# Free bytes between SBUF tiles: other offsets modulo 512 bytes between the moving tiles and the weights of a float32r transformer trunk

## The chip, the core and the metric

The kernel runs on one core of one Trainium2 chip. The metric is the device time of one execution in microseconds (us). Times are medians over repeated executions; one execution is also recorded by the hardware profiler, and all rows below come from that one.

## The reference

Two layers of a transformer trunk over 256 latent tokens and 256 context tokens, model width 1024, float32. Each layer is a half-step SwiGLU feed-forward, an attention (layer 0 differential attention, layer 1 GQA with normed queries and keys), and a second half-step feed-forward; a conditioning vector shifts, scales and gates every branch. Cut to what matters:

```python
def swiglu(h, w_in, w_out):                       # w_in 1024 x 5632, w_out 2816 x 1024
    gate, up = jnp.split(h @ w_in, 2, axis=-1)
    return (jax.nn.silu(gate) * up) @ w_out

for i in range(2):
    mod = (silu(c) @ w_mod[i] + b_mod[i])         # 9 vectors of 1024, also for the context
    x  = x + 0.5 * mod[2] * swiglu(modulate(x, norm_g[i, 0], mod[0], mod[1]), w_ffn_in[i, 0], w_ffn_out[i, 0])
    xc = ...                                      # the same for the context tokens
    h  = modulate(x, norm_g[i, 1], mod[3], mod[4])
    x  = x + mod[5] * attention_i(h, hc)          # 0: differential, 1: GQA
    x  = x + 0.5 * mod[8] * swiglu(modulate(x, norm_g[i, 2], mod[6], mod[7]), w_ffn_in[i, 1], w_ffn_out[i, 1])
return rms_norm(x, final_g)
```

In layer 1 the context stops after the attention, so the last feed-forward has 256 tokens only.

## The kernel before

All 512 tokens lie along the free axis and features along the 128 partitions. Nearly all the work is matrix products on TensorE. Each float32 operand is split into a high part (rounded to float32r) and a low part (the rest), and a product is three float32r matmuls, written by `mac` (lines 384 to 386):

```python
        nc.tensor.matmul(out, ah, bh, start=first, stop=False)
        nc.tensor.matmul(out, ah, bl, start=False, stop=False)
        return nc.tensor.matmul(out, al, bh, start=False, stop=last)
```

The first of the two inputs is the stationary one: 128x128 values loaded into the array by a weight load. The second is the moving one: up to 512 columns that stream through it. The profile writes `gate<-hhi,whi` with the moving tile first. A weight load reads 512 bytes of each partition and runs under the matmul before it; a moving operand of 512 columns reads 2048 bytes of each partition.

The weights come from memory in pieces: `advance` (line 137) loads each into `raw`, ScalarE rounds it to `whi` (line 150), VectorE subtracts to get `wlo` (line 151). They are the stationary operand everywhere but in the value projections, where the normed activations are stationary and the weights move. The kinds of moving tiles are:

- `hhi`, `hlo` (`h_hi`, `h_lo`): the normed input of a stage, 8 tiles of 512 columns each. They feed `gate` and `up` of the feed-forwards, `g` (the first products of a feed-forward) and the projections `qk`, `q`, `k` of the attentions; in `v` they are stationary.
- `ahi`, `alo`: the 11 hidden tiles of one half of a feed-forward. They feed `out`, and `e` at the end of a stage.
- `pa`: attention outputs, which feed `op`.
- `ks`, `kl`: stacked keys, which move against stacked queries `qs` in the scores `sps` (lines 630 and 631).

Products run in the order in which they are written: for each of the 22 column blocks of a feed-forward `gate` and `up` with 8 x 3 matmuls each, then `out` with 11 x 3 matmuls for each pair of output tiles. In differential attention (`diff_attention`, line 674) the tile framework's scheduler interleaves each head's scores, exponentials and transposes with the next head's projections. There `outputs` (line 767) squares the four blocks of a head's output with ScalarE (line 781) into a scratch tile `osq`, of which there is one.

Tiles lie in SBUF in the order in which their pools and tags are first asked for, each pool behind the last, each tile rounded up to 32 bytes. Nothing in the code before fixes an address, and the sizes before `h_hi` are such that, in the built program, weights and moving tiles start at these bytes modulo 512 in each partition (slices of a tile start whole multiples of 512 bytes further on):

| tiles | start modulo 512 before | relative to the weights' 160 |
|---|---|---|
| `whi`, `wlo` | 160 | 0 |
| `hhi`, `hlo` | 160 | 0 |
| `ahi`, `alo` | 32 | 384 |
| `pa` of differential attention | 96 | 448 |
| `kl` / `ks`, `qs` of differential attention | 96 / 352 | 448 / 192 |
| `pa`, `ks`, `kl`, `qs` of GQA | 32 | 384 |

Of the kernel before, what the change touches and what calls it, by code (L numbers as in the profile page):

```python
# [11 lines left out]
F32 = mybir.dt.float32  # L12
F32R = mybir.dt.float32r
# [6 lines left out]
P = 128  # L20
D = 1024
KD = D // P
SEQ = 256
CTX = 256
T = SEQ + CTX
# [18 lines left out]
PIECE_AT = (18, 21, 24, 26, 28, 31, 32, 33)  # L44
WARM = 24


@with_exitstack
def trunk(ctx: ExitStack, tc: tile.TileContext, a: dict):
    nc = tc.nc  # L50
    PSUM = bass.MemoryType.PSUM

    const = ctx.enter_context(tc.tile_pool(name="const", bufs=1))
    wpool = ctx.enter_context(tc.tile_pool(name="wpool", bufs=2))
    stat = ctx.enter_context(tc.tile_pool(name="stat", bufs=1))
    tmp = ctx.enter_context(tc.tile_pool(name="tmp", bufs=3))
# [6 lines left out]
    def ax_tile(name):  # L63
        return ax_ps.tile([P, 512], F32, tag="ax", name=name)


    tok = (slice(0, SEQ), slice(SEQ, T))

    sck = tmp.tile([P, KD, 32], F32, tag="sq", name="sck")
# [65 lines left out]
    def raw_tile(name):  # L135
        return wpool.tile([P, 1024], F32, tag="raw", name=name, bufs=5)

    def advance(upto):
        for i in range(len(ready), min(upto, len(flat) - 1) + 1):
            src, pieces, f = flat[i]  # L140
            parts, c0 = [], 0
            for q, kt in enumerate(pieces):
                n = kt * f
                raw = raw_tile(f"raw{i}_{q}")
                nc.sync.dma_start(raw[:, :n], src[:, c0 : c0 + n])
                hi = wpool.tile([P, 1024], F32R, tag="whi", name=f"whi{i}_{q}", bufs=6)
                lo = wpool.tile([P, 1024], F32R, tag="wlo", name=f"wlo{i}_{q}", bufs=6)
                step = n // 2 if i in fine else n
                for c in (slice(b, b + step) for b in range(0, n, step)):
                    nc.scalar.activation(hi[:, c], raw[:, c], AF.Copy)  # L150
                    nc.vector.tensor_tensor(lo[:, c], raw[:, c], hi[:, c].bitcast(F32), op=ALU.subtract)  # L151
                parts += [(hi[:, k * f : k * f + f], lo[:, k * f : k * f + f]) for k in range(kt)]
                c0 += n
            ready[i] = parts

    def weight(i, look=LOOK):
        advance(i + look)
        return ready[i]
# [165 lines left out]
    def table(func, after):  # L324

        t = tmp.tile([P, 1], F32, tag="tab", name="tab")
        return nc.scalar.activation(t, after, func, scale=0.0, bias=1.0)

    h_hi = [stat.tile([P, T], F32R, name=f"hhi{j}", tag=f"hhi{j}") for j in range(KD)]
    h_lo = [stat.tile([P, T], F32R, name=f"hlo{j}", tag=f"hlo{j}") for j in range(KD)]  # L330

    def modulated_tile(l, n3, s, j, rstd, eng=nc.vector):
# [98 lines left out]
    def boundary(groups, nxt, follow):  # L431


        for s in range(2):
            for i, (outs, ends, tiles) in enumerate(groups):
                ps = [mm_tile(f"e{t}") if t < 3 and not (s and i) else ax_tile(f"e{t}") for t in range(tiles)]
                outs(ps, tok[s])
                if s and i == len(groups) - 1:
                    advance(nxt)
                ends(ps, s)  # L440
            if s:
                advance(nxt + 1)
            steps.extend(modulated(*follow, s))
            if s == 0:
                norm_step()
                norm_step()


    def ffn(l, s, n, follow=None, f_steps=0, o_steps=0, upto=(0, 0)):
# [4 lines left out]
        nxt = base  # L454
        with ExitStack() as st:
            fp = st.enter_context(tc.tile_pool(name=f"ffn{l}{s}", bufs=2))
            a_hi = [fp.tile([P, T], F32R, tag=f"ahi{i}", name=f"ahi{i}", bufs=1) for i in range(NH)]
            a_lo = [fp.tile([P, T], F32R, tag=f"alo{i}", name=f"alo{i}", bufs=1) for i in range(NH)]

            def load_sc(after=None):  # L460
# [33 lines left out]
            for hf in range(2):  # L494
                i0 = 0
                if hf == 0 and opening:
                    i0 = G0
                    with tc.tile_pool(name="open", bufs=2) as sp:
# [7 lines left out]
                        for k in range(KD + 2):  # L506
# [8 lines left out]
                            if k > 1:  # L515
                                w = ready[nxt + k - 2]
# [12 lines left out]
                elif hf == 0:  # L529
                    i0 = 2  # L530
                    banks = [mm_tile(f"g{b}") if b < 3 else ax_tile(f"g{b}") for b in range(4)]
                    w = [weight(nxt, 1), weight(nxt + 1, 0)]
# [15 lines left out]
                for i in range(i0, NH):  # L548
                    w = weight(nxt)
# [9 lines left out]
                for jj in range(0, KD, 2):  # L559
# [18 lines left out]
                    w = [weight(nxt), weight(nxt + 1, 0 if final else LOOK)]  # L578
# [97 lines left out]
    def diff_attention(l):  # L676
        base = start["att", l]
        scale = 64 ** -0.5
        with tc.tile_pool(name="da", bufs=2) as ap:
            lam = ap.tile([P, 4], F32, tag="lam", name="lam", bufs=1)  # L680
            nlam = lam[:, 3:4]
            g1 = ap.tile([P, 1], F32, tag="g1", name="g1", bufs=1)

            lamv = tmp.tile([P, 4, 64], F32, tag="ht", name="lamv")
            for i, n in enumerate(("da_lam_q1", "da_lam_k1", "da_lam_q2", "da_lam_k2")):
                nc.scalar.dma_start(lamv[:, i, :], a[n].to_broadcast([P, 64]))

            kls = [[ap.tile([P, T], F32R, tag=f"kl{i}{m}", name=f"kl{i}{m}", bufs=1) for m in range(2)] for i in range(2)]
            for kl in kls:
                zero_others(kl)  # L690

            def lambdas(after):
                lj = ap.tile([P, 64], F32, tag="lj", name="lj", bufs=1)
                for i in range(2):
                    nc.vector.tensor_tensor_reduce(
                        out=lj, in0=lamv[:, 2 * i, :], in1=lamv[:, 2 * i + 1, :], op0=ALU.mult, op1=ALU.add,
                        scale=1.0, scalar=0.0, accum_out=lam[:, i : i + 1],
                    )
                table(AF.Exp, after)
                nc.scalar.activation(lam[:, 0:2], lam[:, 0:2], AF.Exp)  # L700
                nc.vector.tensor_tensor(lam[:, 2:3], lam[:, 1:2], lam[:, 0:1], op=ALU.subtract)
                nc.vector.tensor_scalar(nlam, lam[:, 2:3], -LAM_INIT, None, op0=ALU.add)
                nc.vector.tensor_scalar(g1, subln_g, 1.0 - LAM_INIT, None, op0=ALU.mult)

            pa = [[ap.tile([P, T], F32R, tag=f"pa{i}{k}", name=f"pa{i}{k}", bufs=1) for k in range(4)] for i in range(2)]

            def v_mac(ps, w, k, s_, t):
                c = slice(s_ * 256 + t * P, s_ * 256 + t * P + P)
# [58 lines left out]
            def outputs(hd):  # L767
                ops = ax_tile("ops")
                h = hd["h"]
                for u in range(4):  # L770
                    k0 = 0 if u < 2 else 2
                    for kt in range(k0, 4):
                        nc.tensor.matmul(
                            ops[:, u * P : u * P + P], hd["pT"][u][:, kt - k0, :],
                            hd["v"][:, kt, (h % 2) * P : (h % 2) * P + P], start=kt == k0, stop=kt == 3,
                        )
                o, ms = hd["o"], hd["ms"]
                nc.vector.tensor_copy(o[:, :, h % 2, :], ops.rearrange("p (t f) -> p t f", t=4))
                for u in range(4):
                    osq = ap.tile([P, P], F32, tag="osq", name="osq", bufs=1)  # L780
                    nc.scalar.activation(
                        osq, ops[:, u * P : u * P + P], AF.Square, accum_out=ms[:, u, h % 2 : h % 2 + 1]
                    )
# [26 lines left out]
            def behind(hd, u):  # L810

                turned(hd, u)
                if u == U_AT and done:
                    pair = done.pop()
                    scaled(pair)
                    h = pair["h"]
                    if h < HEADS // 2:
                        parts_of(pair, o_hi[h - 1 : h + 1], o_lo[h - 1 : h + 1])
                    else:
                        late.append(pair)  # L820
                if u == 3:
                    outputs(hd)
                    if hd["h"] % 2:
                        normed(hd)
                        done.append(hd)
# [44 lines left out]
            for s_ in range(2):  # L870
# [5 lines left out]
                for k in range(KD):  # L876
                    for g in range(2):
                        mac(
                            qkps[g][:, tok[s_]], w_part(wqk, k, slice(g * P, g * P + P)), h_part(k, tok[s_]),
                            k == 0, k == KD - 1,  # L880
                        )
            lambdas(last_norm["rstd"][:, 0:1])
            v_tile(0)
            for t in range(2):
# [27 lines left out]
    def gqa(l):  # L912
        base = start["att", l]
        scale = 64 ** -0.5
        with tc.tile_pool(name="gq", bufs=2) as ap:
            qs = [ap.tile([P, SEQ], F32R, tag=f"qs{i % 8}", name=f"qs{i}", bufs=1) for i in range(16)]
            ks = [ap.tile([P, T], F32R, tag=f"ks{i}", name=f"ks{i}", bufs=1) for i in range(4)]
            kl = [ap.tile([P, T], F32R, tag=f"kl{i}", name=f"kl{i}", bufs=1) for i in range(4)]
# [3 lines left out]
            pa = [[ap.tile([P, SEQ], F32R, tag=f"pa{i}{k}", name=f"pa{i}{k}", bufs=1) for k in range(8)] for i in range(2)]  # L922
# [136 lines left out]
            for n, un in enumerate(units + [None, None]):  # L1059
                if un:  # L1060
                    flight.append((un, weights_of(*un)))
                if n in Q_AT:
                    i, g = divmod(Q_AT.index(n), 2)
# [8 lines left out]
                if n in sqs:  # L1072
                    i, sq = sqs[n]
# [11 lines left out]
            out_proj(base + 8, range(4, 8), o_part, l, SEQ, 1, (l, 2))  # L1085

    ffn(0, 0, T, (0, 1), 2, 1, (0, 7))
    diff_attention(0)
    ffn(0, 1, T, (1, 0), 1.5, 1, (1, 1))
    ffn(1, 0, T, (1, 1), 1.5, 1, (1, 8))  # L1090
    gqa(1)
    ffn(1, 1, SEQ)

# [102 lines left out]
```

## Time and profile before

| | us |
|---|---|
| median of 2 runs | 1729.39 (1728.10 to 1730.68) |
| the profiled execution, its time | 1729.97 |
| its span, first to last instruction | 1727.8 |
| TensorE matmuls busy | 1707.0 |
| VectorE busy | 1159.4 |
| ScalarE busy | 730.3 |
| granted share of the TensorE clock | 0.996 |

Busy times of matmuls overlap, since each is recorded from its start until its last result, while the next has already begun. So the pace of TensorE is read from the distance between the starts of neighbouring matmuls, in the timeline view, and not from the duration of one. Below, "step" means that distance. The timeline's columns are start (us), duration (us), engine, line, operation, output and inputs, shape, and in brackets idle time before it with what ended it.

### The profile page before, as it was taken

The page shows a single profiled execution, that of the slowest core. Times are in us where ns is not written, and L with a number is a line of the kernel's source. Part 1 is how long each engine was busy: PE and PEld are TensorE (multiplying, and loading weights), DVE is VectorE, ACT ScalarE, POOL GpSimd, SP SyncE. Part 2 cuts the span into 40 slices and gives each one's busy share as a digit, 9 for nine tenths or more (in the row PEclk, how much of TensorE's full clock was granted, in tenths as well). Part 3 has the DMA queues.
Part 4 walks back from the last instruction along what each step waited for, and adds up shares of the span by engine and source line. Part 5 has one row for each costly group of instructions (what it writes and reads, how often), then busy time and mean ns, then how long its engine had stood idle before and what let it go on. Part 6 is the DMA issues. An engine that isn't in the chain of part 4 may idle for free.

```text
span 1727.8 us, 24899 instructions
## 1 busy us (share of the span) xinstructions
PE 1707.0 (99%) x9586; PEld 1463.1 (85%) x9586; DVE 1159.4 (67%) x2113; ACT 730.3 (42%) x1359; POOL 26.3 (2%) x42
## 2 busy tenths in 40 slices
PE   9999999999999999999999999999999999999998
PEld 6788888789888889888888898888888897799998
DVE  3697777756888868756766557545543488876664
ACT  3432222235767646322222244222222368765454
POOL 0000000000100000000000000000000010000000
PEclk8999999999999999999999999999999999999999
DMA  7675565442122223545644535546552332145652
GB/s 255 228 242 160 187 215 161 153 151 101 57 67 74 73 74 123 179 140 160 203 156 150 169 110 183 152 132 196 178 160 77 118 101 72 50 164 146 217 162 83
DMA packets 76870, 249.59 MB, mean 144 GB/s; under 512 B 9936, under 2 KB 10064, under 8 KB 76752
## 3 DMA queue, kind: packets, MB, share of 16 engines
q1 hardware_dynamic: 75456, 247.25, 44.9%
q8 instruction: 75, 1.23, 0.3%
q10 hardware_dynamic: 1296, 0.76, 0.1%
q14 instruction: 43, 0.35, 0.1%
HBM read 246.92 MB, written 1.05 MB: 144 GB/s over the span
## 4 chain that ended last, share of the span: by engine, by line
PE 84%; DVE 7%; issue 3%; DMA 2%; ACT 2%; POOL 0%; DVEq 0%; ACTq 0%; POOLq 0%
PE out L385 7%; PE out L386 7%; PE out L384 7%; PE gate L384 7%; PE gate L385 7%; PE gate L386 7%; PE up L385 7%; PE up L386 7%; PE up L384 7%; DMA wm<-in_w_mod 2%; PE g L384 2%; PE g L385 2%; PE g L386 2%; DVE junk L172 1%; PE e L384 1%
## 5 line engine op out<-in xcount | busy, mean ns | idle before, releaser
L150 ACT ACTIVATE whi<-raw 128x1024 fp32r<-128x1024 f32 (+3 forms) x426 | 350.4, 836 | 455.7 <-PE out L385 248.5
L151 DVE TENSOR_TENSOR wlo<-raw,whi 128x1024 fp32r<-128x1024 f32 (+3 forms) x426 | 399.6, 946 | 186.5 <-ACT whi L150 185.7
L172 DVE CUSTOM_DVE_ANT_0 junk<-wm,sc,b_mod 128x1024 bf16<-128x1024 f32 x224 | 287.4, 1283 | 186.4 <-DMA wm<-in_w_mod 182.8
L384 PE MATMUL gate<-hhi,whi 128*128 128x512 f32 (+1 forms) x648 | 234.0, 361 | 0.7 <-DVE av L474 0.7
L386 PE MATMUL gate<-hhi,wlo 128*128 128x512 f32 (+1 forms) x648 | 233.7, 361 | 0.0
L385 PE MATMUL gate<-hlo,whi 128*128 128x512 f32 (+1 forms) x648 | 233.6, 361 | 0.0
L385 PE MATMUL up<-hlo,whi 128*128 128x512 f32 (+1 forms) x648 | 233.6, 361 | 0.0
L384 PE MATMUL up<-hhi,whi 128*128 128x512 f32 (+1 forms) x648 | 233.6, 360 | 0.0
L386 PE MATMUL up<-hhi,wlo 128*128 128x512 f32 (+1 forms) x648 | 233.5, 360 | 0.0
L385 PE MATMUL out<-alo,whi 128*128 128x512 f32 (+1 forms) x638 | 232.3, 364 | 0.0
L384 PE MATMUL out<-ahi,whi 128*128 128x512 f32 (+1 forms) x638 | 232.0, 364 | 0.0
L386 PE MATMUL out<-ahi,wlo 128*128 128x512 f32 (+1 forms) x638 | 231.8, 364 | 0.0
L402 ACT ACTIVATE ahi<-av 128x512 fp32r<-128x512 f32 (+1 forms) x88 | 50.7, 578 | 211.8 <-DVE av L474 204.5
L384 PEld LDWEIGHTS gate<-hhi,whi 128*128 128x128 f32 x648 | 122.4, 189 | 20.2 <-DVE av L474 1.6
L385 PEld LDWEIGHTS out<-alo,whi 128*128 128x128 f32 x638 | 119.9, 188 | 21.4 <-DVE alo L403 0.4
L386 PEld LDWEIGHTS gate<-hhi,wlo 128*128 128x128 f32 x648 | 122.4, 189 | 18.4
L385 PEld LDWEIGHTS up<-hlo,whi 128*128 128x128 f32 x648 | 122.4, 189 | 18.4
L384 PEld LDWEIGHTS up<-hhi,whi 128*128 128x128 f32 x648 | 122.4, 189 | 18.4
L386 PEld LDWEIGHTS up<-hhi,wlo 128*128 128x128 f32 x648 | 122.4, 189 | 18.3
L385 PEld LDWEIGHTS gate<-hlo,whi 128*128 128x128 f32 x648 | 122.4, 189 | 18.2
L386 PEld LDWEIGHTS out<-ahi,wlo 128*128 128x128 f32 x638 | 119.7, 188 | 21.1
L384 PEld LDWEIGHTS out<-ahi,whi 128*128 128x128 f32 x638 | 119.8, 188 | 21.0
(240 smaller groups left out, 2618.0 us busy)
## 6 DMA issues: line engine op xcount, KB each, us to landing
raw<-in_w_in SPq DMA_DIRECT2D x170, 512.0 KB, 4.4
wm<-in_w_mod SPq DMA_DIRECT2D x128, 512.0 KB, 4.2
raw<-in_w_out SPq DMA_DIRECT2D x64, 384.0 KB, 3.4
raw<-in_w_out SPq DMA_DIRECT2D x64, 320.0 KB, 3.1
raw<-in_da_vqk SPq DMA_DIRECT2D x24, 512.0 KB, 3.9
wf<-in_w_mod SPq DMA_DIRECT2D x16, 512.0 KB, 5.0
raw<-in_gq_qkv SPq DMA_DIRECT2D x12, 512.0 KB, 3.8
raw<-in_da_o SPq DMA_DIRECT2D x8, 512.0 KB, 3.7
```

What stands on the lines that cost most here:

```text
L150: nc.scalar.activation(hi[:, c], raw[:, c], AF.Copy)
L151: nc.vector.tensor_tensor(lo[:, c], raw[:, c], hi[:, c].bitcast(F32), op=ALU.subtract)
L172: nc.vector.tensor_tensor_reduce(out=junk, in0=raw, in1=mod_pool["sc"][:, s, :], op0=ALU.mult, op1=ALU.add, scale=1.0, scalar=b_mod[:, l, ...
L384: nc.tensor.matmul(out, ah, bh, start=first, stop=False)
L385: nc.tensor.matmul(out, ah, bl, start=False, stop=False)
L386: return nc.tensor.matmul(out, al, bh, start=False, stop=last)
L402: nc.scalar.activation(hi, src, AF.Copy)
```

## The change

`gap` allocates a tile that nothing uses. Such free bytes go in front of `h_hi` (256) and `h_lo` (320), in front of `ahi` (128) and `alo` (64) in each feed-forward, and in front of `kl` (32) and the second list of `pa` (64) in differential attention. To make the pools' other tiles not disturb the sums, `lam` and `g1` move from the attention's pool to the general pool `tmp`, the small scratch tile `lj` takes the place of `sw`, and `osq` becomes a slice of `sq`, of which there are three.

```diff
+GAPS = dict(const=0, w=0, norm=(256, 320), ffn=(128, 64), da=(32, 64), gq=0)
...
+    def gap(pool, i, n):
+
+        if n:
+            pool.tile([P, n // 4], F32, tag=f"gap{i}", name=f"gap{i}", bufs=1)
...
+    lam = tmp.tile([P, 4], F32, tag="lam", name="lam", bufs=1)
+    nlam = lam[:, 3:4]
+    g1 = tmp.tile([P, 1], F32, tag="g1", name="g1", bufs=1)
+
+    gap(stat, 0, GAPS["norm"][0])
     h_hi = [stat.tile([P, T], F32R, name=f"hhi{j}", tag=f"hhi{j}") for j in range(KD)]
+    gap(stat, 1, GAPS["norm"][1])
     h_lo = [stat.tile([P, T], F32R, name=f"hlo{j}", tag=f"hlo{j}") for j in range(KD)]
...
+            gap(fp, 0, GAPS["ffn"][0])
             a_hi = [fp.tile([P, T], F32R, tag=f"ahi{i}", name=f"ahi{i}", bufs=1) for i in range(NH)]
+            gap(fp, 1, GAPS["ffn"][1])
             a_lo = [fp.tile([P, T], F32R, tag=f"alo{i}", name=f"alo{i}", bufs=1) for i in range(NH)]
...
-            lam = ap.tile([P, 4], F32, tag="lam", name="lam", bufs=1)
-            nlam = lam[:, 3:4]
-            g1 = ap.tile([P, 1], F32, tag="g1", name="g1", bufs=1)
...
+            gap(ap, 0, GAPS["da"][0])
...
-                lj = ap.tile([P, 64], F32, tag="lj", name="lj", bufs=1)
+                lj = ap.tile([P, 1, SEQ], F32, tag="sw", name="lj", bufs=1)[:, 0, 0:64]
...
-            pa = [[ap.tile([P, T], F32R, tag=f"pa{i}{k}", name=f"pa{i}{k}", bufs=1) for k in range(4)] for i in range(2)]
+            pa = []
+            for i in range(2):
+                if i:
+                    gap(ap, 1, GAPS["da"][1])
+                pa.append([ap.tile([P, T], F32R, tag=f"pa{i}{k}", name=f"pa{i}{k}", bufs=1) for k in range(4)])
...
-                    osq = ap.tile([P, P], F32, tag="osq", name="osq", bufs=1)
+                    osq = tmp.tile([P, 256], F32, tag="sq", name="osq")[:, 0:P]
```

The weights stay at 160. The moving tiles then start, modulo 512 and relative to the weights:

| tiles | start modulo 512 after | relative to the weights |
|---|---|---|
| `hhi` | 416 | 256 |
| `hlo` | 224 | 64 |
| `ahi` | 288 | 128 |
| `alo` | 352 | 192 |
| `pa` of differential attention, high / low parts | 192 / 256 | 32 / 96 |
| `kl` / `ks`, `qs` of differential attention | 192 / 256 | 32 / 96 |
| `pa`, `ks`, `kl`, `qs` of GQA | 160 | 0 |

The number of matmuls and their shapes stay the same, and their order does outside differential attention. There the scheduler moves some rows. ScalarE's rows where head 0's output is squared (`osq`), among the exponentials `pe` of head 1 and the transposes `pT`, before:

```order
L746 ACTIVATE pe,ls<-sps,mx 128x512
L781 ACTIVATE osq,ms<-ops 128x128 x2
L746 ACTIVATE pe,ls<-sps,mx 128x512
L781 ACTIVATE osq,ms<-ops 128x128
L746 ACTIVATE pe,ls<-sps,mx 128x512
L781 ACTIVATE osq,ms<-ops 128x128
L718 ACTIVATE qk_3985<-qk 128x512
```

and after:

```order
L766 ACTIVATE pe,ls<-sps,mx 128x512
L801 ACTIVATE osq,ms<-ops 128x128 x4
L766 ACTIVATE pe,ls<-sps,mx 128x512 x2
L738 ACTIVATE qk_3991<-qk 128x512
```

The four squares now stand together, and the two exponentials of head 1's second block of queries behind them; the same happens in each head but the last. TensorE's rows in head 1, where transposes `tps` and `otps` and scores `sps` stand among the projection `qk` for head 2, before:

```order
L762 MATMUL tps<-ident,pe 128x128 x4
L384 MATMUL qk<-hhi_125,whi_0_3898 128x512
L385 MATMUL qk<-hlo_133,whi_0_3898 128x512
L386 MATMUL qk<-hhi_125,wlo_0_3899 128x512
L803 MATMUL otps<-ident,o 128x128 x8
L630 MATMUL sps<-ks_4001,qs_3999 128x256
```

and after:

```order
L782 MATMUL tps<-ident,pe 128x128 x4
L823 MATMUL otps<-ident,o 128x128 x8
L648 MATMUL sps<-ks_4007,qs_4005 128x256
L649 MATMUL sps<-kl_3277,qs_4005 128x256
L648 MATMUL sps<-ks_4008,qs_4006 128x256
L649 MATMUL sps<-kl_3278,qs_4006 128x256
L400 MATMUL qk<-hhi_128,whi_0_3904 128x512
```

One group of three `qk` matmuls moved from ahead of the transposes `otps` to behind the scores; the same happens in one other head, and a few `op` matmuls change places at the attention's end. VectorE computes `g1` (`g<-subln_g`, line 703 before, 719 after) early in the first feed-forward and no longer at the start of the attention, since its tile no longer waits for the attention's pool:

```order
L161 TENSOR_TENSOR wlo_1_616<-raw_1_613,whi_1_615 128x1024
L719 TENSOR_SCALAR g_126<-subln_g 128x1
L492 TENSOR_TENSOR av<-g_203,sg 128x512
```

These are VectorE's rows after; before, the middle one was not there.

More of the change, by code (lines that the diff above doesn't have):

```diff
@@ L64, in ax_tile @@
         return ax_ps.tile([P, 512], F32, tag="ax", name=name)
+    gap(const, 0, GAPS["const"])
     tok = (slice(0, SEQ), slice(SEQ, T))
@@ L146, in advance @@
                 hi = wpool.tile([P, 1024], F32R, tag="whi", name=f"whi{i}_{q}", bufs=6)
+                if i == q == 0:
+                    gap(wpool, 0, GAPS["w"])
                 lo = wpool.tile([P, 1024], F32R, tag="wlo", name=f"wlo{i}_{q}", bufs=6)
@@ L915, in gqa @@
         with tc.tile_pool(name="gq", bufs=2) as ap:
+            gap(ap, 0, GAPS["gq"])
             qs = [ap.tile([P, SEQ], F32R, tag=f"qs{i % 8}", name=f"qs{i}", bufs=1) for i in range(16)]
```

## The prediction

> **What bounds the kernel.** I read the page's busy times and its chain of waits first, then the waits by instruction, then the groups with the shapes kept apart, and last the timeline of single matmuls, since only that shows their pace.
>
> ```profile
> span 1727.8 us, 24899 instructions
> PE 1707.0 (99%) x9586; PEld 1463.1 (85%) x9586; DVE 1159.4 (67%) x2113; ACT 730.3 (42%) x1359; POOL 26.3 (2%) x42
> PE 84%; DVE 7%; issue 3%; DMA 2%; ACT 2%; POOL 0%; DVEq 0%; ACTq 0%; POOLq 0%
> ACT whi L150 <- PE out L385: 248.5, 105, 3.5
> ```
>
> TensorE (PE) is busy for 99% of the span and makes 84% of the chain that ended last. The last row says that ScalarE's rounding of weights waits 248.5 us in all for `out` products to free a weight buffer: the supply of weights runs ahead and TensorE sets the pace. So the time is the number of matmuls times their step, and the question is whether an address alters a step. The counts, from the groups by shape (each row is one of the three lines of `mac`, so every count stands for three times as many matmuls):
>
> ```profile
> L384 PE MATMUL gate<-hhi,whi 128*128 128x512 f32 x472 | 184.1, 390 | 0.7 <-DVE av L474 0.7
> L384 PE MATMUL up<-hhi,whi 128*128 128x512 f32 x472 | 183.7, 389 | 0.0
> L384 PE MATMUL qk<-hhi,whi 128*128 128x512 f32 x112 | 43.9, 392 | 0.0
> L384 PE MATMUL g<-hhi,whi 128*128 128x512 f32 x48 | 20.6, 440 | 0.4 <-ACT hhi L342 0.4
> L384 PE MATMUL k<-hhi,whi 128*128 128x512 f32 x16 | 6.4, 401 | 0.0
> L384 PE MATMUL out<-ahi,whi 128*128 128x512 f32 x462 | 182.5, 395 | 0.0
> L384 PE MATMUL op<-pa,whi 128*128 128x512 f32 x32 | 12.8, 401 | 0.0
> L384 PE MATMUL gate<-hhi,whi 128*128 128x258 f32 x176 | 49.9, 284 | 0.0
> L384 PE MATMUL up<-hhi,whi 128*128 128x258 f32 x176 | 49.9, 283 | 0.0
> L384 PE MATMUL v<-whi,hhi 128*128 128x256 f32 x160 | 45.5, 285 | 0.0
> L384 PE MATMUL g<-hhi,whi 128*128 128x256 f32 x128 | 35.5, 286 | 0.0
> L384 PE MATMUL out<-ahi,whi 128*128 128x256 f32 x176 | 49.5, 283 | 0.0
> ```
>
> Their mean durations hide the pace, because each includes the way through the array under the next one. The pace stands in the timeline; here are the first and the last row of five stretches without a stall:
>
> ```profile
> 699.66 0.39 PE L386 MATMUL up<-hhi,wlo 128*128 128x512 f32 x1
> ...
> 719.83 0.39 PE L385 MATMUL up<-hlo,whi 128*128 128x512 f32 x1
> 344.61 0.40 PE L384 MATMUL out<-ahi,whi 128*128 128x512 f32 x1
> ...
> 364.92 0.39 PE L384 MATMUL out<-ahi,whi 128*128 128x512 f32 x1
> 620.12 0.40 PE L385 MATMUL op<-pa,whi 128*128 128x512 f32 x1
> ...
> 624.79 0.39 PE L384 MATMUL op<-pa,whi 128*128 128x512 f32 x1
> 1559.77 0.28 PE L386 MATMUL up<-hhi,wlo 128*128 128x258 f32 x1
> ...
> 1574.89 0.28 PE L386 MATMUL gate<-hhi,wlo 128*128 128x258 f32 x1
> 1602.74 0.28 PE L386 MATMUL out<-ahi,wlo 128*128 128x256 f32 x1
> ...
> 1616.98 0.28 PE L386 MATMUL out<-ahi,wlo 128*128 128x256 f32 x1
> ```
>
> The first pair spans 90 rows, 89 steps in 20.17 us: 226.6 ns, with the moving tile at offset 0 to the weights. The second spans 88 rows, 87 steps in 20.31 us: 233.4 ns, at offset 384. The third spans 21 rows, 20 steps in 4.67 us: 233.5 ns, at offset 448. All three have the same shape and type. With half the columns the order turns round: 127 rows or 126 steps in 15.12 us are 120.0 ns at offset 0, and 121 rows or 120 steps in 14.24 us are 118.7 ns at offset 384 (the 258 and 256 columns differ by less than 1%). So before the change the steps sort by offset: 226.6 at zero, 233.4 to 233.5 at two others, 6.8 ns apart. How a wide stretch begins at offset 0 says more:
>
> ```profile
> 321.66 0.39 PE L385 MATMUL gate<-hlo,whi 128*128 128x512 f32 x1
> ...
> 322.82 0.39 PE L384 MATMUL gate<-hhi,whi 128*128 128x512 f32 x1
> 323.05 0.39 PE L385 MATMUL gate<-hlo,whi 128*128 128x512 f32 x1
> ...
> 324.86 0.39 PE L384 MATMUL gate<-hhi,whi 128*128 128x512 f32 x1
> ```
>
> After a change of the moving tile the first 5 steps take 1.16 us, 232 ns each; the 8 steps from 323.05 to 324.86 take 1.81 us, 226.3 each. [...]
>
> **The wide products on `hhi` and `hlo`.** They lose offset 0 and go to 256 and 64. Neither offset has a row before. The nearest below is offset 0 itself (226.6, no cost), the nearest above 384 and 448 (233.4). I take 233.4, because both nonzero offsets that can be seen agree within 0.1 ns, though their tiles and stages share nothing. `gate` and `up` are 3 x (472 + 472) = 2832 matmuls; 2832 x 6.8 ns = +19.3 us, wholly on the path. Bounds: 0 to +19.3. If only `hhi` matters (two of the three lines), +12.9; if only `hlo`, +6.4.
>
> `qk`, `g` and `k` are 3 x (112 + 48 + 16) = 528 wide matmuls on the same tiles, in shorter stretches that are cut by scores or waits, so part of them run at 232 already. I take half: 528 x 6.8 / 2 = +1.8 us, bounds 0 and +3.6.
>
> **The narrow products on the same tiles.** `gate`, `up`, `v` and `g` are 3 x (176 + 176 + 160 + 128) = 1920. By the row at offset 384 they gain 1.3 ns each: -2.5 us. Bounds -2.5 and 0.
>
> **`out` and `op`.** They go from 384 and 448 to 128 and 192, 32 and 96. From nonzero to nonzero I take 0; below, the fast step would give (1386 + 96) x 6.8 ns = -10.1 us; above, narrow `out` (528) at 120.0 would give +0.7. GQA goes to offset 0, with narrow products alone, where 1.3 ns each makes tenths of a microsecond.
>
> **`osq` in `sq`'s three buffers.** The scheduler now puts four squares ahead of both exponentials, where three stood ahead of the second. Head 1 before:
>
> ```profile
> 461.92 0.28 ACT L781 ACTIVATE osq<-ops 128x128 f32<-128x128 f32 x1 [2.35 <-DVE o L778]
> 462.32 0.28 ACT L781 ACTIVATE osq<-ops 128x128 f32<-128x128 f32 x1
> 463.50 0.70 ACT L746 ACTIVATE pe<-sps,mx 128x512 f32<-128x512 f32 x1
> 464.32 0.17 DVE L750 RECIPROCAL ls<-ls 128x2 f32<-128x2 f32 x1 [1.23 <-ACT pe L746]
> 465.10 0.75 DVE L752 SCALAR_TENSOR_TENSOR pe<-pe,ls 128x512 f32<-128x512 f32 x1
> 466.25 0.27 PE L762 MATMUL tps<-ident,pe 128*128 128x128 f32 x1
> ```
>
> One more square (0.40 us from start to start) comes before the second exponential, so VectorE's `pe` ends at 466.25 in place of 465.85: exactly when TensorE asks for it. The cover is the 0.40 us of `qk` products between. I cost it at 0; were that cover gone, it would be up to 0.40 us for 8 heads, +3.2. In the two heads where a k-step of `qk` (three matmuls) goes behind the scores the same matmuls run, only later: 0.
>
> **`lam`, `g1`, `lj`.** The multiply into `g1` moves up VectorE's queue to the first feed-forward, in front of a `av` that waits anyway:
>
> ```profile
> 73.37 1.29 DVE L474 TENSOR_TENSOR av<-g,sg 128x512 f32<-128x512 f32 x2 [6.41 <-ACT sg L472]
> L90 SPq DMA_DIRECT2D subln_g<-in_da_subln_g x1: 760/760/760, 52.8 to 52.8; - x1
> DMA to landing us min/median/max: 7.8/7.8/7.8
> L703 DVE TENSOR_SCALAR g<-subln_g x1: 148/148/148, 411.0 to 411.0; 128x1 f32<-128x1 f32 x1
> ```
>
> Its input is issued at 52.8 and lands 7.8 us later, at 60.6; VectorE idles 6.41 us until 73.37, and the operation takes 0.148 us: hidden, 0. Were its input late, `av` and the next `out` would wait for it; with 12 us to spare I leave that out. No queue issues another transfer, and the gaps issue nothing.
>
> **The sum.** +19.3 + 1.8 - 2.5 + 0 = +18.6 us. On the profiled execution's 1729.97 that is 1748.6; on the median of 1729.39, which lies 0.6 below it, 1748.0.
>
> [...] The rows split equal matmuls by offset, 226.6 against 233.4 ns. [...]
>
> **Rivals.** *No effect.* Something other than the offset separates `out` and `op` from `gate` (how their results are grouped, or what the engines beside write), so `h` keeps 226.6: 1729 to 1736, the upper end if `hlo` alone slows. For it: a cause by address is seen only as a sorting of three kinds, never on one kind at two offsets. Against it: `out` and `op` share neither tiles nor neighbours, yet agree; the narrow shapes sort the same way, with the other sign.
>
> *Faster.* Fast steps are common and 384 and 448 are the bad places: `h` stays, `out` and `op` gain 10.1 us: 1719. For it: at offset 0 the fast step has to be found first, so it may be no property of zero. Against: with two samples of two slow, a common fast step is unlikely. For over 2% (34.6 us) every wide step of 4842 would also have to fall another 5.1 ns ((34.6 - 10.1) / 4842), below 221.5; one more unit of 6.8 ns would give 1729.4 - 10.1 - 32.9 = 1686. No row has such a step.
>
> [...]
>
> **How the numbers follow.** `h` slows to 233.4: 52 in 100, 1748, its own range 1742 (`hhi` alone) to 1754 (narrow products gain nothing, and `osq` costs 3.2). No effect: 24, about 1731. Faster within 2%: 12, 1719. Over 2% faster: 3, 1686. Over 2% slower: 9, 1772. The 2% are about what a measurement of this kernel can tell from no change. A range of 1716 to 1758 holds all but the last two cases, some 12 to 14 in 100; it can't be cut at the low end without the third case. Faster 0.03, same 0.88, slower 0.09.
>
> **What would show it.** Right: in the changed kernel's timeline the steps of `gate` and `up` are 233 to 234 ns in stretches of 80 and more, those of `out` stay at 233.4, narrow ones on `hhi` fall to 118.7, ScalarE's waits for `out` stay long and `tps` follows `qk` without idle time. Wrong: `gate` at 226.6 (no effect), `out` at 226.6 (fast steps are common), any step above 237 or below 222, or idle time ahead of `tps`. If the steps are as I say and the time is not, the waits of TensorE moved and not its pace.

## The result and the profile after

| | before | after |
|---|---|---|
| median of 2 runs, us | 1729.39 (1728.10 to 1730.68) | 1742.33 (1741.67 to 1742.98) |
| ratio, 95% interval | 1 | 1.0077 (1.0057 to 1.0097) |
| span of the profiled execution, us | 1727.8 | 1740.8 |

The changed kernel takes 12.9 us longer, 0.8%: inside the range, within 2%, and 5.7 us below the single number. The page of the changed kernel, its span, its busy times and the engines of its chain:

```profile
span 1740.8 us, 24904 instructions
PE 1720.3 (99%) x9586; PEld 1464.8 (84%) x9586; DVE 1160.2 (67%) x2113; ACT 732.0 (42%) x1359; POOL 26.1 (1%) x42
PE 91%; DVE 4%; ACT 3%; issue 2%; DMA 0%; POOL 0%; SPq 0%; DVEq 0%; ACTq 0%; POOLq 0%
```

The same 9586 matmuls are busy 13.3 us longer (1720.3 against 1707.0) and the span is 13.0 us longer: in sum the time went into TensorE's pace and not into its waits. Groups of the changed kernel, shapes apart, one of the three lines of `mac` for each (busy us, mean ns of one, then idle time before them):

```profile
L400 PE MATMUL up<-hhi,whi 128*128 128x512 f32 x472 | 185.9, 394 | 0.0
L400 PE MATMUL gate<-hhi,whi 128*128 128x512 f32 x472 | 185.9, 394 | 0.0
...
L400 PE MATMUL out<-ahi,whi 128*128 128x512 f32 x462 | 180.3, 390 | 0.0
L400 PE MATMUL gate<-hhi,whi 128*128 128x258 f32 x176 | 50.7, 288 | 0.0
...
L400 PE MATMUL v<-whi,hhi 128*128 128x256 f32 x160 | 45.3, 283 | 0.0
```

Against the same line before, `gate` and `up` with 512 columns grew from 390 and 389 to 394 ns, `out` fell from 395 to 390; with 258 columns `gate` grew from 284 to 288, `v` fell from 285 to 283. The other two lines can differ: those of `out` are at 394 and 393 now, those of `gate` with 258 columns at 283 and 286. For the pace itself, the first and last row of four stretches without a stall in the timeline of the changed kernel:

```profile
694.79 0.40 PE L402 MATMUL up<-hhi,wlo 128*128 128x512 f32 x1
...
734.92 0.40 PE L401 MATMUL up<-hlo,whi 128*128 128x512 f32 x1
...
347.69 0.39 PE L400 MATMUL out<-ahi,whi 128*128 128x512 f32 x1
...
374.96 0.39 PE L401 MATMUL out<-alo,whi 128*128 128x512 f32 x1
...
1559.77 0.29 PE L402 MATMUL up<-hhi,wlo 128*128 128x258 f32 x1
...
1583.72 0.29 PE L400 MATMUL up<-hhi,whi 128*128 128x258 f32 x1
...
502.92 0.28 PE L400 MATMUL v<-whi,hhi 128*128 128x256 f32 x1
...
508.45 0.28 PE L402 MATMUL v<-whi,hlo 128*128 128x256 f32 x1
```

`gate` and `up`: 173 steps in 40.13 us, 232.0 ns, where it was 226.6. `out`: 118 steps in 27.27 us, 231.1, where it was 233.4. `gate` and `up` with 258 columns: 196 steps in 23.95 us, 122.2, where it was 120.0. `v`: 47 steps in 5.53 us, 117.7, where the mean was 119.8. So all four changed their pace, and not in one direction.

Below, "mean step" of a kind is taken over all its starts in a trace, leaving out those more than 25 ns above the median, which are stalls.

### The profile page after: what moved, and what is told of

Same layout as the page of the kernel before. It is cut to its first block, busy times and chain, and to the rows that moved or that the text cites. A ratio compares the mean times of both kernels' runs of the same rounds, so it can differ in the third digit from the quotient of the medians.

```text
span 1740.8 us, 24904 instructions
## 1 busy us (share of the span) xinstructions
PE 1720.3 (99%) x9586; PEld 1464.8 (84%) x9586; DVE 1160.2 (67%) x2113; ACT 732.0 (42%) x1359; POOL 26.1 (1%) x42
## 4 chain that ended last, share of the span: by engine, by line
PE 91%; DVE 4%; ACT 3%; issue 2%; DMA 0%; POOL 0%; SPq 0%; DVEq 0%; ACTq 0%; POOLq 0%
PE gate L402 8%; PE up L402 8%; PE gate L400 8%; PE up L400 8%; PE up L401 7%; PE gate L401 7%; PE out L401 7%; PE out L402 7%; PE out L400 7%; PE g L400 2%; PE g L401 2%; PE g L402 1%; PE e L400 1%; PE qk L401 1%; PE qk L400 1%
## 5 line engine op out<-in xcount | busy, mean ns | idle before, releaser
L400 PEld LDWEIGHTS gate<-hhi,whi 128*128 128x128 f32 x648 | 122.2, 189 | 20.7
L400 PEld LDWEIGHTS out<-ahi,whi 128*128 128x128 f32 x638 | 119.9, 188 | 21.0
L401 PEld LDWEIGHTS out<-alo,whi 128*128 128x128 f32 x638 | 119.9, 188 | 20.7 <-DVE alo L419 0.4
```

## The experiments

Apart from e12, all kernels here are the changed kernel with other free bytes. Their instructions and the order of these on every engine are the same (e11 moves one input inside its tiles); only addresses differ. The weights lie at 160 in all but e4, where they lie at 192. In the diffs the line of the changed kernel, `GAPS = dict(const=0, w=0, norm=(256, 320), ffn=(128, 64), da=(32, 64), gq=0)`, is not repeated. Offsets are to the weights, modulo 512.

### e1: the moved tiles without the new offsets

```diff
+GAPS = dict(const=0, w=0, norm=(0, 0), ffn=(448, 0), da=(0, 0), gq=448)
```

> The moved small tiles and the changed order in differential attention, with gaps that put hhi, hlo at 0, ahi, alo at 384 and pa of both attentions at 448 and 384 relative to the weights, as in the kernel before. My theory (the addresses make the whole difference): 1729, within 3, gate and up step 226.7 ns, out 233.3. Rival (the moves cost part of the 12.9 us): 1732 to 1742 with the same steps and idle time ahead of tps or op.

Measured: 1727.24, ratio to the kernel before 0.9985 (0.9975 to 0.9994). Mean steps 226.7 and 233.3, as before. The moved tiles did not cost anything, they gained some 2.6 us; so the new offsets alone cost 1742.33 - 1727.24, about 15 us.

### e2: the offsets of `h` and `a` exchanged

```diff
+GAPS = dict(const=0, w=0, norm=(384, 0), ffn=(192, 0), da=(128, 0), gq=64)
```

> hhi, hlo at 384 and ahi, alo at 0, the offsets of before exchanged; pa as before. Theory that the offset sets the step: gate and up go to 233.3 (2832 x 6.6 ns = +18.7, qk, g, k up to +3), out to 226.7 (1386 x 6.6 = -9.1), narrow gate, up, v, g, q to 118.7 (-2.5), narrow out to 120.0 (+0.7): 1729 + 9 to 11 = 1738 to 1740. Rival (the kind of product sets the step): steps as before, 226.7 and 233.3, and 1729.

Measured: 1737.33, ratio 1.0042 (1.0027 to 1.0057), a little below what was expected, which had left out the 2.6 us of the moved tiles. Two stretches of its timeline, `gate` and `up`, then `out`:

```profile
694.78 0.39 PE L402 MATMUL gate<-hhi,wlo 128*128 128x512 f32 x1
...
734.99 0.39 PE L401 MATMUL up<-hlo,whi 128*128 128x512 f32 x1
...
345.67 0.39 PE L400 MATMUL out<-ahi,whi 128*128 128x512 f32 x1
...
374.92 0.39 PE L400 MATMUL out<-ahi,whi 128*128 128x512 f32 x1
```

The first are 173 steps in 40.21 us, 232.4 ns (233.1 over all), the second 129 steps in 29.25 us, 226.7. The paces changed sides with the addresses: `gate` and `up` went from 226.7 to 233.1 ns, `out` from 233.3 to 226.7, with the same products. The rival "no effect" falls. Nor did work of VectorE or ScalarE beside TensorE make the difference here: of the steps of `gate` and `up` in this trace, the 623 with both idle for over 95% of the step have a mean of 233.4 ns, and the 1036 with VectorE alone at work for over 95% of it 233.0.

### e3: all moving tiles at 0

```diff
+GAPS = dict(const=0, w=0, norm=(0, 0), ffn=(64, 0), da=(64, 0), gq=64)
```

> All moving tiles at 0 to the weights. Theory that the offset sets the step: out at 226.7 (-9.1), op at 226.7 (-0.6), narrow out and e at 120.0 (+1.2): 1729 - 8.5 = 1720 to 1721. Rival (kind sets the step): 1729.

Measured: 1718.77, ratio 0.9935 (0.9920 to 0.9950), a little below what was expected. `out` in its timeline:

```profile
339.96 0.39 PE L400 MATMUL out<-ahi,whi 128*128 128x512 f32 x1
...
374.87 0.39 PE L401 MATMUL out<-alo,whi 128*128 128x512 f32 x1
```

These are 154 steps in 34.91 us, 226.7 ns, which is also the mean step of `out` in this trace. With the 2.6 us of the moved tiles this kernel is 11.1 us faster than the one before.

### e4: everything 32 bytes further on

```diff
+GAPS = dict(const=32, w=0, norm=(0, 0), ffn=(448, 0), da=(0, 0), gq=448)
```

> Weights and all moving tiles 32 bytes further on, so that they start at a multiple of 64 in place of 32 past one; relative offsets as before. If only the offset to the weights counts: 1729, steps 226.7 and 233.3. If the absolute start modulo 64 counts: other steps in gate and up by some multiple or part of 6.7 ns, 3 ns on 4700 wide products being 14 us.

Measured: 1727.97, ratio 0.9987 (0.9978 to 0.9997), mean steps 226.7 and 233.3, the same as e1. So moving both operands by 32 bytes left the steps as they were. With e8 below, where only one moves, they are 6.7 ns apart.

### e5 to e8 and e10: a survey, both parts of a kind at the same offset

The five lines stand for e5 (`h` at 64, `a` at 256), e6 (128 and 192), e7 (320 and 448), e8 (32 and 96) and e10 (160 and 224, and GQA's tiles at 192):

```diff
+GAPS = dict(const=0, w=0, norm=(64, 0), ffn=(256, 0), da=(0, 0), gq=0)
+GAPS = dict(const=0, w=0, norm=(128, 0), ffn=(128, 0), da=(448, 0), gq=448)
+GAPS = dict(const=0, w=0, norm=(320, 0), ffn=(192, 0), da=(256, 0), gq=256)
+GAPS = dict(const=0, w=0, norm=(32, 0), ffn=(128, 0), da=(32, 0), gq=32)
+GAPS = dict(const=0, w=0, norm=(160, 0), ffn=(128, 0), da=(416, 0), gq=96)
```

> hhi, hlo at 64 and ahi, alo at 256 to the weights, pa of both attentions at 0. Theory that zero alone is the fast place: gate, up and out at 233.3 ns, 1719 + 18.7 + 2.0 + 9.1 - 3 = 1746. Rival (each offset has its own step): the changed kernel, with hhi at 256 and hlo at 64, lay at 232.0, so one of these two may lie below 232, and the time at 1735 to 1745; below 226.7 for either would be a faster kernel than any so far.

> hhi, hlo at 128 and ahi, alo at 192. Theory that zero alone is fast: 233.3 in both, 1746. Rival (each offset its own step): the changed kernel's out, with ahi at 128 and alo at 192, lay at 231.1, so one of the two is at most 231.1, and the time is below 1743.

> hhi, hlo at 320 and ahi, alo at 448. Theory that zero alone is fast: 233.3 in both, 1746. Rival: 448 as in op before, 233.3, and 320 anything from 220 to 240, 1709 to 1765.

> hhi, hlo at 32 and ahi, alo at 96. Theory that zero alone is fast: 233.3 in both, 1746. [...]

> hhi, hlo at 160, ahi, alo at 224, pa, ks, kl and qs of GQA at 192. These are the two places modulo 256 (in steps of 32) that no run has had. If only 0 and 64 are below 232: both 233.3 and about 1745, less what narrow products gain; narrow op at 192 at 115 ns as narrow out was there, against 119.6 at 0 (192 x 4.6 = 0.9 us). Rival: one of the two is as 64 (228.9) or lower, 1733 or below.

Measured, one execution each: e5 1720.91, e6 1744.25, e7 1728.14, e8 1745.40, e10 1747.94 (the kernel before beside them 1728.13, beside e10 1729.98). The two stretches of e5, `gate` and `up` at 64, then `out` at 256:

```profile
694.67 0.39 PE L402 MATMUL up<-hhi,wlo 128*128 128x512 f32 x1
...
734.95 0.39 PE L401 MATMUL gate<-hlo,whi 128*128 128x512 f32 x1
...
341.20 0.40 PE L400 MATMUL out<-ahi,whi 128*128 128x512 f32 x1
...
374.80 0.39 PE L401 MATMUL out<-alo,whi 128*128 128x512 f32 x1
```

At 64 they are 176 steps in 40.28 us, 228.9 ns; at 256 148 steps in 33.60 us, 227.0. The theory that zero alone is the fast place fell here. e5's rival, 1735 to 1745, was 14 us too slow as well, since it took the 232.0 of the changed kernel for a step that its two places have alone. e6's rival failed in the same way: neither 128 nor 192 is below 231.1. e8 has 233.3 at 32 and at 96, the step of 128 and 192 within 0.6 ns. e10 came out 3 us above its expectation, with 160 slower than the 233.3 assumed. All offsets together, mean step of products with 512 columns:

| offset modulo 256 | mean step, ns | seen at |
|---|---|---|
| 0 | 226.7 | 0 (`h` before, `out` in e3); 226.9 at 256 (`out` in e5) |
| 32 | 233.3 | 32 (`h` in e8) |
| 64 | 228.9 | 64 (`h` in e5), 320 (`h` in e7) |
| 96 | 233.3 | 96 (`out` in e8) |
| 128 | 232.7 to 233.3 | 128 (`h` in e6), 384 (`h` in e2, `out` before) |
| 160 | 234.3 | 160 (`h` in e10) |
| 192 | 233.3 | 192 (`out` in e6), 448 (`out` in e7) |
| 224 | 233.3 | 224 (`out` in e10) |

Offsets 256 bytes apart gave nearly the same step in all four pairs that were tried: 226.7 and 226.9 ns at 0 and 256, 228.9 twice at 64 and 320, 232.7 and up to 233.3 at 128 and 384, 233.3 twice at 192 and 448. One place is fast (226.7), one is 2.2 ns slower, six are 6.0 to 7.6 ns slower. That it is the offset between the operands and not the start of the moving one is seen by e4 beside e8, at 226.7 and 233.4 ns. In both `hhi` and `hlo` start at 192 modulo 512; the weights start at 192 in e4 and at 160 in e8. `gate` and `up`, e4, then e8:

```profile
694.67 0.39 PE L401 MATMUL gate<-hlo,whi 128*128 128x512 f32 x1
...
734.79 0.39 PE L401 MATMUL gate<-hlo,whi 128*128 128x512 f32 x1
...
699.69 0.40 PE L402 MATMUL gate<-hhi,wlo 128*128 128x512 f32 x1
...
734.93 0.39 PE L400 MATMUL up<-hhi,whi 128*128 128x512 f32 x1
```

The first are 177 steps in 40.12 us, 226.7 ns, the second 151 steps in 35.24 us, 233.4. For products of 256 columns the table looks different: `out` had 119.9 at 0 and 120.0 at 256, 119.9 at 96, 118.7 at 384, 118.3 at 224, 116.9 at 448 and 114.8 at 192, and GQA's `op` at 192 had 114.3 in e10. `v` comes near this row when the offset is counted from its stationary tile, which is `h`, to its moving one, the weights: with `h` at 64 in e5 that is 448, and `v` had 115.2; with `h` at 320 in e7 it is 192, and 115.6; at 96 (e10) it had 119.9, at 224 (e8) 118.3. Other narrow kinds fit less well: `qk` of 256 columns had 115.5 with `h` at 64. `out` with 256 columns in e6:

```profile
1614.79 0.28 PE L402 MATMUL out<-ahi,wlo 128*128 128x256 f32 x1
...
1635.53 0.28 PE L402 MATMUL out<-ahi,wlo 128*128 128x256 f32 x1
```

That stretch is 183 steps in 20.74 us, 113.3 ns, half of 226.7 for half the columns: the lowest step of the narrow products is as low for each column as that of the wide ones, and was seen at 192 in place of 0.

### e9: unequal parts, from places that are fast alone

```diff
+GAPS = dict(const=0, w=0, norm=(256, 256), ffn=(64, 64), da=(64, 0), gq=64)
```

> hhi at 256 and hlo at 0; ahi at 0 and alo at 64; pa of both attentions at 0. If offsets count modulo 256 (64 and 320, 0 and 256 gave the same steps) and unequal offsets of the two moving parts cost by themselves: gate and up at 226.7, for 256 and 0 are then the same place, and out at 232.0 as gate in the changed kernel with 256 and 64: 1719 + 1386 x 5.3 ns = 1726. Rival (each moving tile pays its own offset, and mixing costs nothing): out at the mean of two 226.7 and one 228.9, 227.4, time 1720; rival (the hi and lo parts must lie alike modulo 512): gate also near 232, 1741.

Measured: 1724.07 in one execution (before beside it 1729.98). `gate` and `up` with `hhi` at 256 and `hlo` at 0, then `out` with `ahi` at 0 and `alo` at 64:

```profile
694.75 0.39 PE L401 MATMUL up<-hlo,whi 128*128 128x512 f32 x1
...
734.87 0.39 PE L401 MATMUL gate<-hlo,whi 128*128 128x512 f32 x1
...
341.44 0.39 PE L400 MATMUL out<-ahi,whi 128*128 128x512 f32 x1
...
374.84 0.40 PE L400 MATMUL out<-ahi,whi 128*128 128x512 f32 x1
```

177 steps in 40.12 us are 226.7 ns: 256 and 0 together have the step of 0 alone. 144 steps in 33.40 us are 231.9 (232.0 over all), the step of `gate` in the changed kernel, where the parts lie at 256 and 64, and not 227.4, the mean of the places' own steps (two thirds at 226.7, one third at 228.9). So the unequal offsets 0 and 64 cost 4.6 ns above that mean here, and 0 and 256, at 226.7, again gave one step.

### e11: narrow products at 192

The last feed-forward's hidden tiles and GQA's tiles move to 192, and its normed input is written and read 48 columns (192 bytes) into its tiles:

```diff
+GAPS = dict(const=0, w=0, norm=(0, 0), ffn=(64, 0), last=(256, 0), da=(64, 0), gq=256)
+HS = 48
...
+        nc.scalar.activation(h_hi[j][:, HS : HS + SEQ], x[j][:, :SEQ], AF.Copy, scale=g)
...
+            gap(fp, 0, GAPS["last" if n == SEQ else "ffn"][0])
...
+                    hcols = slice(HS, HS + WIDE) if n == SEQ else cols
```

> All moving tiles of 512 columns at 0 to the weights; in the last feed-forward, whose products have 256 or 258 columns, ahi, alo at 192 and the normed input 48 columns (192 bytes) into its tiles, and GQA's pa, ks, kl, qs at 192. Theory that wide and narrow products have different fast places: wide as with all at 0 (226.7), narrow out at 114.8 in place of 119.9 (528 x 5.1 ns = 2.7 us), op at 114.5 in place of 119.6 (192 x 5.1 = 1.0), gate and up with 258 columns at 115 to 119 in place of 120.8 (1056 x 2 to 6 = 2.1 to 6.3): 1718.8 - 6 to 10 = 1709 to 1713. Rival (the two columns more undo it): gate and up at 120 to 122, 1714 to 1717.

Measured: 1717.05, ratio 0.9929 (0.9916 to 0.9943), an interval that overlaps e3's. The expected 1709 to 1713 was missed; 1717 is at the end of what the rival gave. `gate` and `up` stayed at 120.8, as with all at 0, so 258 columns did not gain at 192. GQA's `op` came to 116.5, where it had 114.3 at the same 192 in e10, and `out` came to 115.7 in the mean, because part of it ran as here:

```profile
1589.81 0.28 PE L401 MATMUL out<-ahi,whi 128*128 128x256 f32 x1
...
1610.19 0.28 PE L403 MATMUL out<-ahi,wlo 128*128 128x256 f32 x1
```

173 steps in 20.38 us are 117.8 ns, at the offset and with the shape that gave 113.3 in e6. Within one execution it varies too: the first and the second half of `out` have means of 113.4 and 116.2 in e6, and 117.3 and 114.1 in e11. So at one offset two stretches, of 183 and of 173 steps, kept 113.3 and 117.8 ns; what decides between them was not found.

### e12: `osq` alone

```diff
-                    osq = ap.tile([P, P], F32, tag="osq", name="osq", bufs=1)
+                    osq = tmp.tile([P, 256], F32, tag="sq", name="osq")[:, 0:P]
```

This is the kernel before with that one edit; weights and moving tiles keep their addresses.

> The kernel before with one edit: osq is a slice of sq, of which there are three. All weights and moving tiles stay where they were before. With all the moves and the offsets of before the time was 1727.2 against 1729.9, interval of the ratio 0.9975 to 0.9994. If the reordering by osq makes that difference: 0.9975 to 0.9994 again, and the first gap of op near 0.8 us in place of 1.7. If the early g1 and lam make it, or chance in the late weights of the modulation: 1.000, and 1.7 us.

Measured: 1727.21 against 1729.37, ratio 0.9989 (0.9980 to 0.9998). So `osq` makes most or all of the gain of e1. TensorE's and ScalarE's rows stand in the order of the changed kernel here, so the whole reordering of these two comes from `osq`. The clearest place in the traces is TensorE's turn from `op` to the last head's scores. Before:

```profile
599.22 0.40 PE L385 MATMUL op<-pa,whi 128*128 128x512 f32 x1
600.93 0.50 PE L630 MATMUL sps<-ks,qs 128*128 128x512 f32 x1 [1.32 <-ACT ks L625]
```

And with three buffers for `osq`:

```profile
597.00 0.40 PE L385 MATMUL op<-pa,whi 128*128 128x512 f32 x1
597.79 0.50 PE L630 MATMUL sps<-ks,qs 128*128 128x512 f32 x1 [0.39 <-ACT ks L625]
```

The gap from start to start falls from 1.71 to 0.79 us, because ScalarE's and VectorE's new order has the keys `ks` ready earlier: the idle time that they end falls from 1.32 to 0.39 us. The rest of the 2 us is spread: 0.7 us in stalls of `qk`, 0.4 us in `otps`, and 1 us at one `gate` product that waited for VectorE, and VectorE for a late modulation weight, in the execution recorded before. No trace of e1, e2, e4 or e12 has that wait; whether it was chance, one recorded execution can't tell.

## Why the prediction was right, and where its terms were off

**The bound and the mechanism** were as said: TensorE's pace sets the time, the pace depends on where the moving tile lies relative to the weights (226.7 to 234.3 ns for the wide products over the offsets tried), and the moved tiles, the one other part of the change, took 2.2 to 2.6 us off (e12, e1). e2 shows it with the paces exchanged (233.1 and 226.7), e4 and e8 with one start of the moving tile and two of the weights (226.7 and 233.4). But none of the three steps came out as forecast under "Right": `gate` and `up` have 232.0 and not 233 to 234, `out` did not stay, and narrow `gate` and `up` rose.

**The wide products on `hhi` and `hlo`** were the main term, +19.3 us at 6.8 ns. The right sign, too large: from 226.7 in e1 to 232.0 in the changed kernel they are 2832 x 5.3 ns = +14.9 us. The step that failed is the choice "I take 233.4, because both nonzero offsets that can be seen agree". 256 had 226.9 where 0 had 226.7, and 64 cost 2.2 ns, so by the survey neither tile is at a slow place. The 232.0 came with the two parts at unequal places, which the prediction had not thought of: at 256 and 64 here, and again at 0 and 64 in e9. That the forecast still had the right sign is luck in this step: with both parts at 64 and the hidden tiles at 256, e5 was faster than the kernel before, 1720.91 against 1728.13. The bound "if only `hhi` matters, +12.9" equals the measured total by coincidence.

**`qk`, `g` and `k`**: +1.8 forecast; `qk` measures +1.2, wide `g` +0.4 and `k` +0.2 against e1.

**Narrow products**: -2.5 forecast, by the row at 384. `v` (-0.9), `g` (-0.6) and `q` (-0.3) fell, but `gate` and `up` with 258 columns rose from 120.4 to 122.1, 1056 x 1.7 ns = +1.8. Together near 0: the term failed by taking one offset's row for all. It also took `v` as if `h` were its moving tile; there the weights move.

**`out`**: 0 forecast, bounds -10.1 and +0.7. It fell from 233.3 to 231.1, 1386 x 2.2 ns = -3.0. Alone, 128 and 192 gave 232.7 and 233.3, so here the unequal parts took 1.6 to 2.2 ns less. Why was not settled. Narrow `out` rose from 118.7 to 119.4, +0.4 us, inside its bound of +0.7.

**The moved tiles**: 0 forecast, up to +3.2; measured -2.2 to -2.6 (e12, e1). The feared place in the changed kernel, head 1's squares and exponentials:

```profile
465.91 0.28 ACT L801 ACTIVATE osq<-ops 128x128 f32<-128x128 f32 x1 [2.35 <-DVE o L798]
...
466.17 0.27 ACT L801 ACTIVATE osq<-ops 128x128 f32<-128x128 f32 x1
...
466.42 0.28 ACT L801 ACTIVATE osq<-ops 128x128 f32<-128x128 f32 x1
...
466.67 0.29 ACT L801 ACTIVATE osq<-ops 128x128 f32<-128x128 f32 x1
...
467.58 0.71 ACT L766 ACTIVATE pe<-sps,mx 128x512 f32<-128x512 f32 x1
...
469.20 0.75 DVE L772 SCALAR_TENSOR_TENSOR pe<-pe,ls 128x512 f32<-128x512 f32 x1
...
470.31 0.60 PE L782 MATMUL tps<-ident,pe 128*128 128x128 f32 x4
```

The squares follow each other every 0.25 us, where with one buffer it was 0.40. So four of them take less time (4 x 0.25) than three did (3 x 0.40), `pe` is ready at 469.95, and TensorE asks for it at 470.31 without idle time. The cover held; the working had priced the added square as if it still waited for the one buffer.

**The sum**: +14.9 + 1.2 + 0.4 + 0.2 (wide `h`), -3.0 + 0.4 (`out`), near 0 (narrow) and -2.2 to -2.6 (moves) make +11.5 to +11.9, against +12.9 measured. The rest lies in groups that were not followed up and in the spread between runs. In the recorded execution of the changed kernel the start is late besides: the first `g` matmul begins at 24.11 us, where it began at 22.25, because TensorE waits longer for VectorE's squares among the products that sum the norms (0.92 and 0.82 us, where it was 0.55 us once). With the same instructions in the same order e4 begins it at 24.30 and e3 at 22.19, so the order of instructions does not make it; what does is open.

**The rivals.** "No effect" is refuted by e2 and e3: with e1 they differ in addresses alone, and they take 1737.3 and 1718.8 us where e1 takes 1727.2. The premise of "faster" is half there: a fast place besides 0 exists (226.9 ns at 256), though modulo 256 only one place of eight is fast, but the change put no kind of wide tile wholly there. "Over 2% slower", 9 in 100 at 1772, rests on a step that no run shows: the highest mean step of `gate`, `up` or `out` in any run is 234.3 ns, in e10, which took 1747.94.

## What to carry to other kernels

Where a trace shows TensorE without gaps, compare the distance between starts for products of equal shape: if it differs between stages, look at the addresses. For float32r products of 512 columns with a weight load for each, lay all moving tiles at a whole multiple of 256 bytes from the weights' slices, the high and low parts alike: here the steps were 226.7 to 226.9 ns at these places and 228.9 to 234.3 at the others. All at 0 was worth 0.65% (0.50 to 0.80) over the kernel before, together with three buffers in place of one for a scratch tile, and costs a few free bytes. A single scratch buffer can hold up the engine that fills it, even if nobody reads it: ScalarE's squares followed each other every 0.40 us with one and every 0.25 with three.

## What was not expected of the hardware

- Offsets 256 bytes apart had nearly the same step, where they had been counted modulo 512: 226.7 and 226.9 ns at 0 and 256, 228.9 at both 64 and 320.
- Two places alternating cost more than either alone in one case: 232.0 ns at 0 and 64, where the places have 226.7 and 228.9. At 128 and 192 it was less than either, 231.1 where they have 232.7 and 233.3.
- Products of 256 columns had their lowest step elsewhere (113.3 ns at 192, 119.9 at 0), and at the same place one stretch ran at 113.3 and another at 117.8.
- No run had a steady step below 226.6 ns at 512 columns; offsets finer than 32 bytes, and high and low weights at unequal offsets, were not tried.
